# PE held to program order in the first pair of feature tiles of each SwiGLU, and the first half's norm sums issued behind the third product

## The chip, the cores and the metric

The kernel runs on one core of one Trainium2 chip. The metric is the device time of one execution in microseconds, lower being better. The engines are called PE (matrix multiply, with PEld for its weight loads), DVE (vector), ACT (scalar activation), POOL (GpSimd) and SP, which issues the large DMAs.

## What is computed

Two encoder layers run on 560 columns of activations (512 frames, 32 running frames, 16 meta tokens) with a width of 1024. A mixer (gated linear attention in layer 0, latent attention in layer 1) stands between two half-step SwiGLUs in each layer, so there are four SwiGLUs:

```
def rmsnorm(x, w):
    y = x32 * lax.rsqrt(jnp.mean(x32 * x32, axis=-1, keepdims=True) + RMS_EPS)
    return (y * w.astype(jnp.float32)).astype(x.dtype)

def swiglu_half(h, norm_w, w_gate, w_up, w_down):
    hn = rmsnorm(h, norm_w)
    return h + 0.5 * ((jax.nn.silu(hn @ w_gate) * (hn @ w_up)) @ w_down)
```

There are 2816 features, 22 tiles of 128. All matrices are float32.

## The kernel before, in words

Activations lie transposed in `h` (128 partitions, 8 blocks of the width, 560 columns, in two halves of 280). Every weight comes from HBM as float32, and `split` makes two fp32r tiles of it: ACT casts it to `whi` (L331), DVE subtracts to get `wlo` (L332). `mm` then issues high by high (L378) and low by high (L379) in turn, and high by low (L381) behind them.

`gate_up` makes the gate and up projections of a pair of feature tiles by a Strassen-like scheme with seven products instead of eight. A product is two accumulations of twelve matmuls, 24 in all. In the order of the code the products use the operands b11, b21, t6, t5, t7, t4, b22; the text counts them from first (b11) to seventh (b22). Their weights come from the generator `quads`: four quadrants r11, r12, r21, r22, each loaded by two DMAs of 256 KB into a tile `fr` of six buffers, and sums of them made on DVE (L451). The first and second product use r11 and r12 as they are. The third uses r11 + r21 + r22, for which three additions are issued ahead of its cast; the fourth, fifth and sixth use s1, r21 and r22, and the seventh r12 plus the sum. `whi` and `wlo` have four buffers each. In the second to fourth SwiGLU the split weights of the first two products were made in the stage before (`first_weights`); the two quadrants are loaded a second time for the sums.

The products go to the two-bank PSUM tiles A, B and C. `copy` takes a first result to SBUF on ACT (L490). `finish` combines it with a second one on DVE (L497, L499), multiplies by the norm's factor (L501), takes SiLU on ACT (L503), multiplies gate by up (L504) and splits the result into `ah` and `al`.

The norm's factor is applied late, at `finish`. `roots(hf)` sums the squares of a half over the partitions by six matmuls (L410, three column blocks, each of two passes) and makes the reciprocal root by a chain of eleven small DVE instructions of 128x3, each on the result of the one before (L424, L425, then L430, L431, L432 three times). `scale(hf)`, called by the first `finish` of a half, turns the result into a row by three transposes on PE (L417) and copies it to SBUF on ACT (L272).

`first` is true in the first pair of each SwiGLU. There, in the code before, `roots(0)` is issued ahead of the third product, but behind it where `xs.lazy` is set, which is so in the first SwiGLU alone. `finish(0, 0, ...)`, with `scale(0)`, and `roots(1)` are issued behind the fourth product; `scale(1)` comes with the `finish` behind the fifth.

`ffn` goes over five groups of feature tiles. The first group is one pair; from the second on, the down projection of the group before is woven between the products (`between`, `fill`). In the first pair there is nothing to weave in.

The order that each engine runs is made when the program is built. A planner simulates the engines and puts each instruction that is ready on its engine, in the order in which the code emitted them where several are ready. An engine then runs its list strictly in order. The list on PE can so differ from the code's order, as can the lists on DVE and ACT.

Of the kernel before, what the change touches and what calls it, by code (L numbers as in the profile page):

```python
# [2 lines left out]

# [49 lines left out]
def weight_plan():  # L53
# [3 lines left out]
    def ffn(i, l):  # L57
        for gi, (f0, f1) in enumerate(GROUPS):
# [3 lines left out]
            for m in range(ND):  # L62
                plan.append((("d", i, l, gi, m), f1 - f0))

    ffn(1, 0)
    for h in range(GH):
        plan.extend((("v", h, j), nk * V_COLS[h] / P) for j, nk in enumerate(V_PARTS[h]))
# [4 lines left out]
        if h >= 2:  # L72
            plan.extend((("go", h - 2, c), 8) for c in range(4))
    ffn(2, 0)
    ffn(1, 1)
    for m in range(6):
        plan.append((("wd", m), 8))
# [212 lines left out]
class Net:  # L290
# [176 lines left out]
    def gate_up(self, i, l, f, xs, act, raws, tp, between):  # L467


        nc = self.nc  # L470
        v = nc.vector
        n = xs.n
        left = self.quads(i, l, f, raws, xs.early, xs.left)
        done = []

        def product(to, op, more=False):
            if xs.lazy and op in ("b11", "b21"):
                w, x = next(left), xs.operand(op)
            else:
                x, w = xs.operand(op), next(left)  # L480
            for j in range(2):
                self.mm(to[:, j, :n], w, 4 * j, x, (0, n), more)

        def gap():
            done.append(0)
            between(len(done))

        def copy(of, tag):
            r = tp.tile([P, 2, 280], F32, name="r", tag=tag, bufs=1)
            nc.scalar.copy(r[:, :, :n], of[:, :, :n])  # L490
            return r

        def finish(j, hf, bank, r, how):
            gu = tp.tile([P, 2, 280], F32, name="gu", tag="gu", bufs=2)
            b, r, t = bank[:, :, :n], r[:, :, :n], gu[:, :, :n]
            if how == "neg":
                v.scalar_tensor_tensor(t, b, -1.0, r, op0=ALU.mult, op1=ALU.subtract)  # L497
            else:
                v.tensor_tensor(t, b, r, op=how)  # L499
            y = xs.scale(hf).unsqueeze(1).to_broadcast([P, 2, n])  # L500
            v.tensor_tensor(t, t, y, op=ALU.mult)  # L501
            g, u = gu[:, 0, :n], gu[:, 1, :n]
            nc.scalar.activation(g, g, AF.Silu)  # L503
            v.tensor_tensor(g, g, u, op=ALU.mult)  # L504
            c = slice(*xs.halves[hf])
            self.split(act[j][0][:, c], act[j][1][:, c], g)

        first = not xs.finish
        A = self.bank2("A")
        product(A, "b11")  # L510
        r1 = copy(A, "ra")
        gap()
        C = self.bank2("C")
        product(C, "b21")
        if not first:
            finish(0, 0, C, r1, ALU.add)
        gap()
        if first and not xs.lazy:
            xs.roots(0)
        product(A, "t6", True)  # L520
        r2 = copy(A, "rb")
        gap()
        if first and xs.lazy:
            xs.roots(0)
        B = self.bank2("B")
        product(B, "t5")
        p5 = copy(B, "rc")
        if first:
            finish(0, 0, C, r1, ALU.add)
            xs.roots(1)  # L530
        gap()
        product(A, "t7", True)
        r3 = copy(A, "ra")
        finish(1, 1, A, p5, "neg")
        gap()
        D = self.bank2("C")
        product(D, "t4")
        finish(1, 0, D, r3, ALU.subtract)
        gap()
        product(B, "b22", True)  # L540
        finish(0, 1, B, r2, ALU.add)
        gap()
# [19 lines left out]
    def ffn(self, i, l, xs, halves, side, turn):  # L562


        ap, fw = Pools(self.tc, side), Pools(self.tc, side)
        acp = ap(f"act{i}{l}")
        if xs.lazy:
            free = [acp.tile([P, 2, T // 2], F32, name="xt", tag=f"a{x}{j}") for j in range(4, 8) for x in "hl"]
            xs.tmp = [t[:, k, :] for t in free for k in range(2)]
        raws, tp = fw(f"raw{i}{l}", 6), fw(f"tmp{i}{l}", 1)  # L570
        fill = []
        last = len(GROUPS) - 1
        for gi, (f0, f1) in enumerate(GROUPS):
            j0 = 4 * (gi % 2) if gi < last else 0
            acts = [(acp.tile([P, T], F32R, name=f"ah{j}", tag=f"ah{j}"),
                     acp.tile([P, T], F32R, name=f"al{j}", tag=f"al{j}")) for j in range(j0, j0 + 4 if gi == last else j0 + f1 - f0)]
            slots = [7 * min((f1 - f0) // 2, 2) - 1]

            def between(k):
                if slots[0] <= 0 or (slots[0] == 7 * min((f1 - f0) // 2, 2) - 1 and k < 2):  # L580
                    return
                for _ in range(-(-len(fill) // slots[0])):
                    fill.pop(0)()
                slots[0] -= 1

            for f in range(f0, f1, 2):
                if gi == last and f == f0 + 4:
                    assert not fill
                    acts += [(acp.tile([P, T], F32R, name=f"ah{j}", tag=f"ah{j}"),
                              acp.tile([P, T], F32R, name=f"al{j}", tag=f"al{j}")) for j in range(4, 8)]  # L590
                self.gate_up(i, l, f, xs, acts[f - f0:f - f0 + 2], raws, tp, between)
            assert not fill
            order = [(m, hf) for m in range(ND) for hf in (0, 1)]
            if gi < last:
                fill = self.down(i, l, gi, acts, halves, order)
        fw.close()
        after = turn()
        order = Quads.ORDER if isinstance(after, Quads) else (
            [(0, 0), (1, 0), (0, 1), (1, 1), (2, 0), (3, 0), (2, 1), (3, 1)] + [(m, hf) for hf in (0, 1) for m in range(4, 8)])
        for f in self.down(i, l, last, acts, halves, order, after):  # L600
            f()
        ap.close()
# [967 lines left out]
```

## Time and profile before

| | us |
|---|---|
| median of 3 runs | 2114.17 (2113.75 to 2114.99) |
| profiled execution | 2109.41 |
| its span, first to last instruction | 2107.5 |
| PE busy | 2026.0 (96%) |
| DVE busy | 1643.2 (78%) |
| ACT busy | 1018.4 (48%) |

In a timeline row stand the start, the duration, engine, line, operation, tiles and count; a bracket tells the idle time of the engine before it and what ended it. Matmuls overlap, so the step from start to start is what PE spends on one, not the duration.

### The profile page before, as it was taken

To read this page: it belongs to the slowest core of one execution; us is meant where nothing else is said; L and a number is where in the kernel's file an instruction comes from. 1 tells how busy PE (TensorE), PEld (TensorE's weight loads), DVE (VectorE), ACT (ScalarE), POOL (GpSimd) and SP (SyncE) were. 2 spreads that over 40 slices of the span, in tenths; PEclk is the share of its full clock that TensorE was granted. 3 is DMA by queue.
4 is the path that set the end of the run, shared out by engine and by line. 5 is a ranking of instruction groups with operands and counts; after the bars stand their busy time and mean duration, and the time that the engine had idled before them with its cause. 6 is when DMAs were issued, how large, how long until landed. Compare 5 with 4: busy or idle time off the path is not lost.

```text
span 2107.5 us, 38039 instructions
## 1 busy us (share of the span) xinstructions
PE 2026.0 (96%) x15290; PEld 1980.2 (94%) x15290; DVE 1643.2 (78%) x3097; ACT 1018.4 (48%) x1822; POOL 51.4 (2%) x117
## 2 busy tenths in 40 slices
PE   5999999999999899999989999999999979999997
PEld 5999999989999799999979999999988969999997
DVE  8887878556658888788778877886788788878884
ACT  6444445455445444445545444454575454444451
POOL 0000000101110000000000000000210000000000
PEclk8999999999999899999989999999999989999998
DMA  3323222222221332322222322222211223232221
GB/s 131 106 87 107 93 96 78 77 68 71 73 80 55 108 103 82 106 86 91 81 95 96 105 92 91 95 83 92 61 51 59 71 86 100 90 111 91 96 72 62
DMA packets 93633, 183.29 MB, mean 87 GB/s; under 512 B 10433, under 2 KB 22081, under 8 KB 93457
## 3 DMA queue, kind: packets, MB, share of 16 engines
q1 hardware_dynamic: 89632, 176.24, 26.1%
q10 hardware_dynamic: 3824, 4.63, 0.7%
q8 instruction: 120, 1.97, 0.4%
q14 instruction: 57, 0.46, 0.1%
HBM read 176.84 MB, written 3.99 MB: 86 GB/s over the span
## 4 chain that ended last, share of the span: by engine, by line
PE 82%; DVE 10%; ACT 3%; DMA 2%; issue 2%; SPq 0%; POOL 0%; DVEq 0%; ACTq 0%; POOLq 0%
PE Y L381 8%; PE Y L378 8%; PE Y L379 8%; PE A L379 5%; PE A L381 5%; PE A L378 5%; PE ps L378 4%; PE ps L381 4%; PE ps L379 4%; PE B L378 3%; PE B L379 3%; PE B L381 3%; PE C L379 3%; PE C L381 3%; PE C L378 3%; DVE wlo L332 3%
## 5 line engine op out<-in xcount | busy, mean ns | idle before, releaser
L332 DVE TENSOR_TENSOR wlo<-fr,whi 128x1024 fp32r<-128x1024 f32 x302 | 363.9, 1216 | 17.2 <-ACT whi L331 17.0
L378 PE MATMUL Y<-ah,whi 128*128 128x280 f32 (+1 forms) x1408 | 373.8, 291 | 1.9 <-ACT ah L331 1.0
L379 PE MATMUL Y<-ah,wlo 128*128 128x280 f32 (+1 forms) x1408 | 373.4, 292 | 0.0
L331 ACT CAST whi<-fr 128x1024 fp32r<-128x1024 f32 x302 | 313.3, 1049 | 92.9 <-PE C L381 34.6
L378 PE MATMUL A<-x,whi 128*128 128x280 f32 (+1 forms) x1056 | 286.3, 296 | 29.5 <-ACT whi L331 29.5
L379 PE MATMUL A<-x,wlo 128*128 128x280 f32 (+1 forms) x1056 | 285.7, 296 | 1.0 <-DVE wlo L332 1.0
L378 PEld LDWEIGHTS Y<-ah,whi 128*128 128x128 f32 x1408 | 265.2, 188 | 3.4 <-ACT ah L331 1.7
L556 DVE SCALAR_TENSOR_TENSOR h<-Y,h 128x280 f32<-128x280 f32 (+1 forms) x320 | 140.9, 443 | 161.9 <-PE Y L381 161.2
L379 PEld LDWEIGHTS Y<-ah,wlo 128*128 128x128 f32 x1408 | 265.4, 188 | 0.0
L332 DVE TENSOR_TENSOR wlo<-raw,whi 128x512 fp32r<-128x512 f32 (+5 forms) x237 | 203.6, 861 | 76.7 <-ACT whi L331 71.9
L331 ACT CAST whi<-raw 128x512 fp32r<-128x512 f32 (+5 forms) x237 | 176.0, 744 | 173.4 <-PE ps L381 55.2
L381 PE MATMUL Y<-al,whi 128*128 128x280 f32 (+1 forms) x1408 | 233.9, 292 | 0.0
L378 PEld LDWEIGHTS A<-x,whi 128*128 128x128 f32 x1056 | 203.9, 193 | 31.1 <-ACT whi L331 31.1
L451 DVE TENSOR_TENSOR fr<-fr 128x1024 f32<-128x1024 f32 x176 | 214.5, 1219 | 20.4 <-DMA fr<-W 18.1
L379 PEld LDWEIGHTS A<-x,wlo 128*128 128x128 f32 x1056 | 203.7, 193 | 1.7 <-DVE wlo L332 1.4
L381 PEld LDWEIGHTS Y<-al,whi 128*128 128x128 f32 x1408 | 201.2, 189 | 0.0
L378 PE MATMUL B<-x,whi 128*128 128x280 f32 (+1 forms) x704 | 188.6, 293 | 3.4 <-ACT whi L331 3.4
L379 PE MATMUL C<-x,wlo 128*128 128x280 f32 (+1 forms) x704 | 187.1, 292 | 3.5 <-DVE wlo L332 3.5
L379 PE MATMUL B<-x,wlo 128*128 128x280 f32 (+1 forms) x704 | 187.4, 292 | 0.8 <-DVE wlo L332 0.8
L378 PE MATMUL C<-x,whi 128*128 128x280 f32 (+1 forms) x704 | 187.4, 291 | 0.6 <-ACT whi L331 0.6
L381 PE MATMUL A<-x,whi 128*128 128x280 f32 (+1 forms) x1056 | 181.2, 294 | 0.0
L490 ACT COPY r<-A 128x560 f32<-128x560 f32 (+1 forms) x132 | 82.2, 623 | 174.1 <-PE A L381 173.8
(368 smaller groups left out, 4059.2 us busy)
## 6 DMA issues: line engine op xcount, KB each, us to landing
fr<-W SPq DMA_DIRECT2D x352, 256.0 KB, 3.4
raw<-W SPq DMA_DIRECT2D x80, 512.0 KB, 3.5
raw<-W SPq DMA_DIRECT2D x112, 256.0 KB, 2.9
raw<-W SPq DMA_DIRECT2D x40, 128.0 KB, 2.1
h<-xT SPq DMA_DIRECT2D x3, 560.0 KB, 7.6
raw<-W SPq DMA_DIRECT2D x4, 384.0 KB, 3.1
o_y<-h SPq DMA_DIRECT2D x8, 136.0 KB, 2.2
o_y<-h ACTq DMA_DIRECT2D x8, 136.0 KB, 1.9
```

The costliest lines, as they stand in the source:

```text
L331: self.nc.scalar.copy(hi, src)
L332: self.nc.vector.tensor_tensor(lo, src, hi.bitcast(F32), op=ALU.subtract)
L378: f(hi[:, b0 + k, :], xh[:, c], start=not more and k == 0, stop=False)
L379: f(lo[:, b0 + k, :], xh[:, c], start=False, stop=False)
L381: f(hi[:, b0 + k, :], xl[:, c], start=False, stop=k == n - 1)
L451: add = lambda out, x, y: nc.vector.tensor_tensor(out, x, y, op=ALU.add)
L490: nc.scalar.copy(r[:, :, :n], of[:, :, :n])
L556: nc.vector.scalar_tensor_tensor(self.h[:, m, c], Y[:, :n], 0.5, self.h[:, m, c], op0=ALU.mult, op1=ALU.add)
```

## The change

```
         if not first:
             finish(0, 0, C, r1, ALU.add)
         gap()
-        if first and not xs.lazy:
-            xs.roots(0)
         product(A, "t6", True)
         r2 = copy(A, "rb")
         gap()
-        if first and xs.lazy:
+        if first:
             xs.roots(0)
         B = self.bank2("B")
         product(B, "t5")
...
-                self.gate_up(i, l, f, xs, acts[f - f0:f - f0 + 2], raws, tp, between)
+                with self.tc.manual_schedule(engines={mybir.EngineType.PE}) if f == 0 else nullcontext():
+                    self.gate_up(i, l, f, xs, acts[f - f0:f - f0 + 2], raws, tp, between)
```

`manual_schedule` makes PE run what is emitted inside the block in the order of the code. The other engines' order, and where PE instructions from outside the block fall among those inside, stay with the planner. `f == 0` holds once in each SwiGLU. The second part moves `roots(0)` behind the third product in the second to fourth SwiGLU; in the first it already stood there.

## Rows read from the trace of the kernel before

**Rows 1.** The page: busy time by engine.

```profile
PE 2026.0 (96%) x15290; PEld 1980.2 (94%) x15290; DVE 1643.2 (78%) x3097; ACT 1018.4 (48%) x1822; POOL 51.4 (2%) x117
```

**Rows 2.** The waits of PE over the whole span: what waited for what, us in total, times, longest.

```profile
PE A L378 <- ACT whi L331: 29.5, 6, 8.8
PE Y L417 <- DVE ry L432: 21.4, 8, 3.3
```

**Rows 3.** The timeline of PE, second SwiGLU: the first and second product, the norm's sums, the third and fourth product, and the first product of the second pair.

```profile
678.90 0.29 PE L378 MATMUL A<-x,whi 128*128 128x280 f32 x1
...
682.00 0.29 PE L378 MATMUL C<-x,whi 128*128 128x280 f32 x1
...
685.12 0.72 PE L410 MATMUL Y<-ones,acc 128*128 128x1 f32 x6
...
698.23 0.60 PE L378 MATMUL A<-x,whi 128*128 128x280 f32 x1 [3.76 <-ACT whi L331]
...
704.09 0.29 PE L379 MATMUL B<-x,wlo 128*128 128x280 f32 x1
...
716.31 0.29 PE L378 MATMUL A<-x,whi 128*128 128x280 f32 x1
```

**Rows 4.** The timeline of DVE, second SwiGLU: the three additions for the third product with one for the seventh, the split of the seventh, two additions for the second pair, and the split of its first weights.

```profile
693.37 4.99 DVE L451 TENSOR_TENSOR fr<-fr 128x1024 f32<-128x1024 f32 x4
...
705.89 1.23 DVE L332 TENSOR_TENSOR wlo<-fr,whi 128x1024 fp32r<-128x1024 f32 x1 [3.00 <-ACT whi L331]
708.00 2.48 DVE L451 TENSOR_TENSOR fr<-fr 128x1024 f32<-128x1024 f32 x2 [0.88 <-DMA fr<-W]
710.40 1.22 DVE L332 TENSOR_TENSOR wlo<-fr,whi 128x1024 fp32r<-128x1024 f32 x1
```

**Rows 5.** The window view, second SwiGLU, from just ahead of the issue of the quadrants' DMAs (679.10): stretch, its length, busy us of PE, PEld, DVE, ACT, POOL with counts, mean granted PE clock (1.00 is 2.4 GHz, 0.50 is 1.2 GHz), busy share of the DMA engines, GB/s.

```profile
679.00:687.50 8.50, 6.85 (x55) 6.76 (x53) 7.54 (x20) 4.06 (x7) 0.00 (x0) 1.00 0.81 254
...
679.00:689.00 10.00, 7.12 (x58) 7.04 (x57) 8.50 (x26) 4.06 (x7) 0.00 (x0) 1.00 0.81 261
```

**Rows 6.** The timeline of DVE, third SwiGLU: the first half's combination, then the first and last instruction of each of the two chains of the norm.

```profile
1077.25 0.74 DVE L499 TENSOR_TENSOR gu<-C,r 128x560 f32<-128x560 f32 x1 [1.43 <-PE C L381]
1077.91 0.15 DVE L424 TENSOR_SCALAR rv<-Y 128x3 f32<-128x3 f32 x1
...
1079.86 0.16 DVE L432 SCALAR_TENSOR_TENSOR ry<-rt,ry 128x3 f32<-128x3 f32 x1
1081.22 0.16 DVE L424 TENSOR_SCALAR rv<-Y 128x3 f32<-128x3 f32 x1 [1.20 <-PE Y L410]
...
1084.18 0.15 DVE L432 SCALAR_TENSOR_TENSOR ry<-rt,ry 128x3 f32<-128x3 f32 x1
```

**Rows 7.** The window view, third SwiGLU, columns as in rows 5.

```profile
1076.00:1077.00 1.00, 1.00 (x10) 1.00 (x10) 0.00 (x0) 0.00 (x0) 0.00 (x0) 1.00 0.00 0
...
1089.00:1090.00 1.00, 0.60 (x1) 0.29 (x1) 1.00 (x2) 1.00 (x3) 0.00 (x0) 0.50 0.00 0
```

**Rows 8.** The timeline of PE, third SwiGLU: the first instructions of the third product.

```profile
1089.12 0.60 PE L378 MATMUL A<-x,whi 128*128 128x280 f32 x1 [3.76 <-ACT whi L331]
...
1090.46 0.57 PE L379 MATMUL A<-x,wlo 128*128 128x280 f32 x1
```

**Rows 9.** The timelines of DVE and PE, fourth SwiGLU: the additions and the first matmul of the third product.

```profile
1723.48 5.00 DVE L451 TENSOR_TENSOR fr<-fr 128x1024 f32<-128x1024 f32 x4
...
1728.36 0.59 PE L378 MATMUL A<-x,whi 128*128 128x272 f32 x1 [6.17 <-ACT whi L331]
```

**Rows 10.** The window view, fourth SwiGLU, from just ahead of the issue of the quadrants' DMAs (1713.68), columns as in rows 5.

```profile
1713.00:1722.00 9.00, 3.02 (x16) 2.67 (x15) 5.68 (x26) 2.10 (x3) 0.00 (x0) 0.70 0.78 246
```

**Rows 11.** The timeline of PE, first SwiGLU: the third product, the sums of the first half, the sixth product, and the transposes of the second half.

```profile
24.32 0.60 PE L378 MATMUL A<-x,whi 128*128 128x280 f32 x1 [6.43 <-ACT whi L331]
...
30.96 0.72 PE L410 MATMUL Y<-ones,acc 128*128 128x1 f32 x6
31.54 0.38 PE L379 MATMUL B<-x,wlo 128*128 128x280 f32 x1
...
45.90 0.39 PE L379 MATMUL C<-x,wlo 128*128 128x280 f32 x1 [3.49 <-DVE wlo L332]
46.13 0.49 PE L417 MATMUL Y<-ident,ry 128*128 128x128 f32 x3
46.38 0.38 PE L378 MATMUL C<-x,whi 128*128 128x280 f32 x1
```

**Rows 12.** The window view, first SwiGLU, columns as in rows 5.

```profile
24.00:25.00 1.00, 0.60 (x1) 0.29 (x1) 1.00 (x3) 1.00 (x3) 0.00 (x0) 0.50 0.00 0
...
46.00:47.00 1.00, 1.00 (x9) 1.00 (x10) 1.00 (x3) 0.34 (x1) 0.00 (x0) 1.00 0.12 16
```

**Rows 13.** The timeline of DVE, first SwiGLU: the first and last instruction of the two chains of the norm, and the instruction put behind the first one.

```profile
31.72 0.16 DVE L424 TENSOR_SCALAR rv<-Y 128x3 f32<-128x3 f32 x1 [1.64 <-PE Y L410]
31.80 0.45 DVE L400 TENSOR_TENSOR acc<-acc,sq 128x280 f32<-128x280 f32 x1
...
36.05 0.15 DVE L432 SCALAR_TENSOR_TENSOR ry<-rt,ry 128x3 f32<-128x3 f32 x1
...
38.27 0.15 DVE L424 TENSOR_SCALAR rv<-Y 128x3 f32<-128x3 f32 x1
...
45.76 0.15 DVE L432 SCALAR_TENSOR_TENSOR ry<-rt,ry 128x3 f32<-128x3 f32 x1
```

More of the change, by code (lines that the diff above doesn't have):

```diff
@@ L1 @@
-from contextlib import ExitStack
+from contextlib import ExitStack, nullcontext
 from functools import partial
@@ L517, in gate_up @@
         gap()
-        if first and not xs.lazy:
-            xs.roots(0)
         product(A, "t6", True)
@@ L522, in gate_up @@
         gap()
-        if first and xs.lazy:
+        if first:
             xs.roots(0)
@@ L590, in ffn @@
                               acp.tile([P, T], F32R, name=f"al{j}", tag=f"al{j}")) for j in range(4, 8)]
-                self.gate_up(i, l, f, xs, acts[f - f0:f - f0 + 2], raws, tp, between)
+                with self.tc.manual_schedule(engines={mybir.EngineType.PE}) if f == 0 else nullcontext():
+                    self.gate_up(i, l, f, xs, acts[f - f0:f - f0 + 2], raws, tp, between)
             assert not fill
```

## The prediction

> **What bounds the kernel now.** I read the page first: PE is busy for 96% of the span, DVE for 78% [rows 1]. So the kernel is bound by PE, and a change of order can only win back idle PE time or lose more of it. Next come PE's waits [rows 2]. The largest is for the cast of a third product's weights (29.5 us in six cases, the kernel's start among them), and behind it the transposes of the norm's factor, which wait for DVE's chain (21.4 us in eight cases). Both stand in the first pair of a SwiGLU, where no down projection fills in. The timelines of these stretches then show the order. In the second SwiGLU the second product is issued by 685.12, PE makes the sums of *both* halves, and the third product begins at 698.23 [rows 3]. DVE begins the additions for the third product's weights only at 693.37, when the second chain is over [rows 4]. The planner hoisted the second half's sums, which the code emits behind the fourth product, into the idle PE, and the additions came out behind them in DVE's fixed order. The reader is to see that 13.1 us pass there in which PE does nothing but those sums.
>
> **Part one: the additions come earlier.** With PE in program order and `roots(0)` behind the third product, DVE has no chain to run ahead of the additions. What comes last is then the transfer of the quadrants, or DVE's last work before.
>
> *Second SwiGLU.* Eight transfers of 262 KB, 2.10 MB, are needed. By 687.5 the DMAs moved 8.5 us x 254 GB/s = 2.16 MB, by 689.0 2.61 MB, which is all ten that were issued, the next pair's included [rows 5]. So the data are there between 687.3 and 689.0; with some time for the landing I take 688.6. From the start of the additions to the first matmul the trace has 693.37 to 698.23, 4.86 us (three additions, the cast, two handovers). The third product then begins at 693.5 instead of 698.23: 4.8 us won.
>
> *Third SwiGLU.* The DMAs had long been silent at 1076 [rows 7]. DVE is free when L499 ends, 1077.25 + 0.74 = 1078.0, or 0.1 earlier, since the next instruction overlaps it [rows 6]. 1077.9 + 4.9 = 1082.8 against 1089.12 [rows 8]: 6.3 us won. Were the additions put ahead of L499, which waits 1.43 us for PE, it would be 2 us more.
>
> *Fourth SwiGLU.* The additions start at 1723.48 and the product at 1728.36 [rows 9]. Here the DMAs were issued late: by 1722.0 they moved 9 x 246 = 2.21 MB [rows 10]. The data thus landed hardly before the additions began. I take 0.2 us won, with bounds of 0 and 1.7.
>
> *First SwiGLU.* The sums already stood behind the third product, and PE ran them in nearly that order [rows 11]; the first matmuls hoisted there sat in waits. I take 0, bounds of 1 us either way, since a new plan may move things.
>
> Sum: 11.3 us won.
>
> **Part two: the sums no longer hide in the gap.** They now stand between products, on PE's path. Six L410 cost 31.54 - 30.96 = 0.58 us, three L417 46.38 - 46.13 = 0.25 us [rows 11]. That is 0.83 a half, 1.66 a SwiGLU, and 5.0 us in the second to fourth. The 18 + 9 instructions and their operations are the same as before; only their cover goes.
>
> **Part three: the new wait.** In program order `scale(0)`'s transposes stand behind the fourth product, and everything later on PE is queued behind them: the sums of the second half, then the fifth product, then `scale(1)`'s transposes, then the sixth. Each chain must so be done within one product. A product takes 682.00 - 678.90 = 3.1 us [rows 3]. A chain alone takes 1077.91 to 1080.02, 2.1 us, and one that shares DVE with the first half's `finish` 1081.22 to 1084.33, 3.1 us [rows 6]. Either is just hidden. In the first SwiGLU, where DVE always has other work ready, one larger instruction stands between any two of the chain: 31.72 to 36.20, 4.5 us, and 38.27 to 45.91, 7.6 us [rows 13]. By these rows the stall lies between 0 and 1.4 + 4.5 = 5.9 us a SwiGLU.
>
> What would be ready in the second to fourth? A large instruction put into the chain adds its step of 1.14 us less the 0.12 us that the chain leaves free anyway, so 1.0. While the first chain runs, the split of the seventh product's weights comes up, about 1.8 us behind the third product (704.09 to 705.89) [rows 3, 4]: 2.1 + 1.0 = 3.1, a stall of 0.2 with the handover. While the second runs, the first half's `finish` is due, and the split of the second pair's first weights, which followed the fourth product [rows 4], and perhaps one addition for that pair. 3.1 + 1.0, and half of another 1.0, plus 0.1 for the handover, less 3.1: 1.6. I take 1.8 us a SwiGLU, 5.4 in three. It is nearer to the chain with `finish` than to the first SwiGLU, for the operands of the norm are all made by then.
>
> Here a rule of the Trainium skill is weighed. The row shows that the small instruction at 31.72 lasts 0.16 us, but that the next one starts 0.08 us after it [rows 13]; so interleaving costs DVE only half of it. The Trainium skill (VectorE: DVE Perf Modes, "The DRAIN you can't avoid") says that the next operation does not start until the pipeline is empty, though it leaves room for some that start earlier. By the row, the sum stays. By the rule, read strictly, each of eleven would cost 0.08 us more, 0.9 a chain, 5.3 us in six, and the time would be about 2118.5. The trace contradicts it, so that it gets no chance of its own.
>
> **Clock.** The gap before the third product stays long in the second SwiGLU (685.1 to 693.5) and the fourth, so the restart is at 1.2 GHz as before. In the third it shrinks to about 5.6 us (L499's wait for PE ended at 1077.25 [rows 6]). After a wait of 6.43 us the granted clock was 0.50, after one of 3.49 us still 1.00 [rows 11, 12]; 5.6 lies between. The third product there began at 0.50 [rows 7]. A product behind such a gap took 5.9 us from its start instead of 3.1 [rows 3]; of the 2.8, some are a wait for `wlo`. If the clock held, some 2 us would be won. I take 0.
>
> **Sum.** -11.3 + 5.0 + 5.4 = -0.9 us. The profiled execution took 2109.41 (span 2107.5 and 1.9 around it) and would take 2108.5; it lies 4.8 below the median of the timed runs, and I carry the difference over: 2114.2 - 0.9 = 2113.3. The work behind does not take up the stalls: when the first pair ends, the second pair's first weights were split at 711.6, 4.7 us ahead of their product at 716.31 [rows 3, 4], so neither a later PE nor 2 us more of DVE work makes DVE late.
>
> **The rivals.** 0.2% (4.2 us) is what a measurement of this kernel can tell from no change.
>
> 1. *The chains hide.* If the planner runs both chains with little between them, the stalls vanish: -11.3 + 5.0 = -6.3, 2107.9; with the clock held in the third SwiGLU 2105.8. It decides where the stalls stay under 0.7 us a SwiGLU. For it: outside the first SwiGLU the first chain had nothing put between its instructions. Against it: everything ready is put there in the first.
>
> 2. *The chains are held up, slower.* DVE runs its list in order. If the planner, which reckons with its own landing times, puts the second pair's additions into the first chain, the chain waits for their transfers. In the second SwiGLU these additions waited for DMA until 708.00, 9.8 us behind the third product's start, and took 2.4 [rows 4]. The transposes would then be due at about 12.8, while the fourth product ends at 5.9 + 0.6 + 3.1 = 9.6 [rows 3]: a stall of 3.2, and 1.1 for the second chain. 4.3 in each of three is 12.9: -6.3 + 12.9 = +6.6, 2120.8. It decides where the stalls exceed 3.5 us a SwiGLU. Against it: in the order of the code these additions come last, so they go in only where nothing older is ready.
>
> 3. *The change doesn't do what it says*: the additions stay late, for another reason than the chains. Then only PE's cost remains and the same wait is longer: the sums leave a gap that stays, +5.0 or 2119.2. Against it: nothing else stands on DVE between L499 and the additions but the chains and what hangs on them [rows 6].
>
> **How the numbers follow.** Forecast, little change: 0.57. Rival 1: 0.27. Rival 2: 0.12. Rival 3: 0.04. So faster by over 0.2% 0.27, within 0.2% 0.57, slower 0.16. The predicted time is 2113.3. Its own range goes from 2110 to 2118 (stalls of 0.7 to 3.5 us). To leave out no more than two in ten, the range reaches into both rivals: from 2107, with the stalls hidden and about half the chance of the clock, to 2119.
>
> **What will show it.** Right: the L410 rows of the second to fourth SwiGLU behind the third product's 24 matmuls; the additions directly behind L499 and the landing; the third product some 4.8, 6.3 and 0.2 us earlier against the second one than before; PE's wait for L417 down from 21.4 us to some 7. The step most in doubt is the stall at the second half's transposes. Wrong: a wait of over 3 us at L417 in these three, or none at all; additions that still start as late as before; a gain of 2 us or more in the first SwiGLU, for which I have no reason.

## The result, and the profile after

The changed kernel takes 2122.58 us (median of 17 runs, one of which, at 3066.81 us and a granted clock of 0.60, is left out of the ratio) against 2114.50 for the kernel before (17 runs beside them): a ratio of 1.0036, 95% interval 1.0025 to 1.0046. It is slower by some 8 us. The forecast was 2113.3, between 2107 and 2119; it was wrong, on the side to which 0.16 had been given.

The page of the changed kernel hardly differs from [rows 1]; PE is busy 8.5 us more in a span of 2123.6 us, which is 16.1 us longer than that of the profiled execution before.

```profile
PE 2034.5 (96%) x15290; PEld 1986.9 (94%) x15290; DVE 1643.5 (77%) x3097; ACT 1019.0 (48%) x1822; POOL 51.4 (2%) x117
```

PE's waits, to be held against [rows 2] (what waited for what, us in total, times, longest):

```profile
PE A L378 <- ACT whi L331: 44.0, 5, 14.5
PE Y L417 <- DVE ry L432: 12.4, 9, 3.8
...
PE A L378 <- DVE gu L497: 4.4, 3, 1.5
```

The first row is PE's wait for the third product's cast. It has grown from 29.5 to 44.0 us, although the third product comes earlier: before, the sums and transposes lay inside the gap and cut it into pieces. L417's wait went down from 21.4 to 12.4 us, where the prediction looked for 7. In the second to fourth SwiGLU it is 5.0 us in sum, close to the 5.4 forecast there; 3.8 us stand at the second half's transposes of the first SwiGLU, where PE before waited 3.49 us for a `wlo` instead [rows 11]. The third row is new, and the prediction had nothing for it.

The timeline of PE in the second SwiGLU, the rows that answer to [rows 3] (only rows with a wait, the sums and transposes, and the two matmuls behind the first sums):

```profile
698.72 0.60 PE L378 MATMUL A<-x,whi 128*128 128x280 f32 x1 [8.95 <-ACT whi L331]
700.03 0.60 PE L379 MATMUL A<-x,wlo 128*128 128x280 f32 x1 [0.72 <-DVE wlo L332]
...
704.89 0.72 PE L410 MATMUL Y<-ones,acc 128*128 128x1 f32 x6
705.48 0.38 PE L378 MATMUL B<-x,whi 128*128 128x280 f32 x1
705.69 0.29 PE L379 MATMUL B<-x,wlo 128*128 128x280 f32 x1
...
709.86 0.54 PE L417 MATMUL Y<-ident,ry 128*128 128x128 f32 x3 [1.04 <-DVE ry L432]
710.24 0.73 PE L410 MATMUL Y<-ones,acc 128*128 128x1 f32 x6
...
715.64 0.40 PE L378 MATMUL A<-x,whi 128*128 128x280 f32 x1 [1.49 <-DVE gu L497]
...
719.47 0.51 PE L417 MATMUL Y<-ident,ry 128*128 128x128 f32 x3 [0.46 <-DVE ry L432]
```

The order is the one that was forecast as far as 710.24: third product, sums, fourth product, transposes, sums, fifth product. But PE stops three times behind the third product: at the first transposes, at 715.64, and at the second transposes. The matmul of 715.64 is the first product of the *second pair*. It comes from outside the block that is held to program order, and the planner put it ahead of the second half's transposes. Its bank A has to be read by DVE (L497) first.

The timeline of DVE there answers to [rows 4]:

```profile
690.31 0.73 DVE L499 TENSOR_TENSOR gu<-C,r 128x560 f32<-128x560 f32 x1
693.84 5.00 DVE L451 TENSOR_TENSOR fr<-fr 128x1024 f32<-128x1024 f32 x4 [2.79 <-DMA fr<-W]
...
705.65 0.16 DVE L424 TENSOR_SCALAR rv<-Y 128x3 f32<-128x3 f32 x1 [2.27 <-PE Y L410]
...
707.31 1.22 DVE L332 TENSOR_TENSOR wlo<-fr,whi 128x1024 fp32r<-128x1024 f32 x1
...
708.52 1.22 DVE L451 TENSOR_TENSOR fr<-fr 128x1024 f32<-128x1024 f32 x1
709.65 0.15 DVE L432 SCALAR_TENSOR_TENSOR ry<-rt,ry 128x3 f32<-128x3 f32 x1
709.77 1.23 DVE L451 TENSOR_TENSOR fr<-fr 128x1024 f32<-128x1024 f32 x1
...
711.56 0.15 DVE L424 TENSOR_SCALAR rv<-Y 128x3 f32<-128x3 f32 x1
711.63 1.21 DVE L332 TENSOR_TENSOR wlo<-fr,whi 128x1024 fp32r<-128x1024 f32 x1
...
713.20 1.21 DVE L451 TENSOR_TENSOR fr<-fr 128x1024 f32<-128x1024 f32 x1
...
714.85 0.74 DVE L497 SCALAR_TENSOR_TENSOR gu<-A,r 128x560 f32<-128x560 f32 x1
...
715.79 1.22 DVE L332 TENSOR_TENSOR wlo<-fr,whi 128x1024 fp32r<-128x1024 f32 x1
...
717.05 1.22 DVE L451 TENSOR_TENSOR fr<-fr 128x1024 f32<-128x1024 f32 x1
...
719.16 0.16 DVE L432 SCALAR_TENSOR_TENSOR ry<-rt,ry 128x3 f32<-128x3 f32 x1
```

The additions (693.84) now stand right behind the combination of the first half (690.31) and wait for nothing but their data, as forecast. Then the reader is to see what lies inside the chains. The first (L424 at 705.65 to the end of L432 at 709.80, 4.1 us) holds a split of 1.22 us and an addition for the second pair, and the next addition (709.77) stands ahead of L501. The second runs from 711.56 to 719.32, 7.8 us for eleven instructions that take 2.1 alone: between them lie two splits and two additions of 1.2 us, L497 and more. No row inside the chains has a wait for DMA.

Two marks in each SwiGLU give the account. "End" is the first matmul of the sixth product of the second pair, where the changed order has passed. The times are us from the first matmul of the SwiGLU's first product, read from PE's timeline.

| | third product, before → after | end, before → after | end, difference |
|---|---|---|---|
| second SwiGLU | 19.32 → 15.34 | 58.28 → 60.55 | +2.3 |
| third | 18.35 → 12.00 | 58.05 → 58.18 | +0.1 |
| fourth | 21.71 → 20.63 | 59.97 → 66.17 | +6.2 |

The sum, 8.6 us, agrees with the loss between the medians, 8.1. The two profiled executions differ by 16.1 us; the other 7.5 lie outside these stretches, 1.3 of them in the first SwiGLU. Differences of that size come without a change of order: a2 below, which runs the same instructions in the same order as the kernel before, took 6.6 us more than it in its profiled execution, and no more in these three stretches. The third product did come earlier, by 4.0, 6.4 and 1.1 us, 11.4 in sum; behind it 20.0 us were lost. The next table takes the steps from start to start on PE behind the third product's first matmul apart. A step beyond the full-clock one (0.126 us with 280 columns, 0.1245 with 272) is put down to the instruction that came late; the figures are after less before.

| us, behind the third product's start | second | third | fourth | sum | predicted |
|---|---|---|---|---|---|
| sums and transposes on PE's path | 1.8 | 2.1 | 2.1 | 6.0 | 5.0 |
| stalls: transposes, and the second pair's first product | 3.5 | 3.5 | 3.9 | 10.9 | 5.4 |
| the third product's wait for its `wlo` | 0.4 | 0.4 | 0.4 | 1.1 | 0 |
| all other matmul steps | 0.6 | 0.5 | 0.9 | 2.0 | 0 |

Of the last row 1.1 us are the first matmuls behind sums, transposes and stalls, four in a SwiGLU: their step is 0.21 us or a little more instead of 0.126, at a granted clock of 1.00 (705.48 to 705.69 above). 0.5 us are matmuls at a granted clock of 0.50, and the rest is spread over many steps.

### The profile page after: what moved, and what is told of

It is laid out like the page before. It is cut to its first block, busy times and chain, and to the rows that moved or that the text cites. A ratio compares the mean times of both kernels' runs of the same rounds, so it can differ in the third digit from the quotient of the medians.

```text
span 2123.6 us, 38032 instructions
## 1 busy us (share of the span) xinstructions
PE 2034.5 (96%) x15290; PEld 1986.9 (94%) x15290; DVE 1643.5 (77%) x3097; ACT 1019.0 (48%) x1822; POOL 51.4 (2%) x117
## 4 chain that ended last, share of the span: by engine, by line
PE 84%; DVE 9%; DMA 2%; ACT 2%; issue 2%; SPq 0%; POOL 0%; DVEq 0%; ACTq 0%; POOLq 0%
PE Y L381 8%; PE Y L378 8%; PE Y L379 8%; PE A L379 6%; PE A L381 6%; PE A L378 5%; PE ps L378 4%; PE ps L381 4%; PE ps L379 4%; PE C L379 4%; PE C L378 4%; PE C L381 3%; PE B L379 3%; PE B L381 3%; PE B L378 3%; DVE wlo L332 3%
## 5 line engine op out<-in xcount | busy, mean ns | idle before, releaser
L451 DVE TENSOR_TENSOR fr<-fr 128x1024 f32<-128x1024 f32 x176 | 214.5, 1219 | 28.6 <-DMA fr<-W 25.9
```

Of the source, the lines that this page charges most:

```text
L451: add = lambda out, x, y: nc.vector.tensor_tensor(out, x, y, op=ALU.add)
```

## The experiments

Each ran beside the kernel before on its chip. The sum of the differences at the "end" in the second to fourth SwiGLU, against the profile of before, is given for each as "stretches"; 4.2 us are 0.2%.

| run | stretches, us | ratio to before, 95% interval |
|---|---|---|
| the change | +2.3 +0.1 +6.2 | 1.0036 (1.0025 to 1.0046) |
| a1_order_alone | +1.6 +0.8 +4.9 | 1.0037 (1.0024 to 1.0051) |
| a2_sums_alone | 0.0 -0.3 +0.2 | 1.0005 (0.9994 to 1.0017) |
| a3_not_in_first | | 1.0048 (1.0031 to 1.0065) |
| a4_short_chain | -2.3 -4.9 +2.3 | 0.9990 (0.9979 to 1.0001) |
| d1_paired_chains_behind | 0.0 -3.4 +3.8 | 0.9999 (0.9987 to 1.0011) |
| b1_both_sums_ahead | -2.9 -2.8 +0.5 | 0.9983 (0.9970 to 0.9995) |
| e1_sums_ahead_planned | -0.4 0.0 +0.2 | 1.0000 (0.9987 to 1.0012) |
| c4_short_chain_on_before | -1.2 -1.6 +0.5 | 0.9986 (0.9974 to 0.9998) |
| g1_one_chain_behind_additions | -3.0 -5.2 +1.0 | 0.9958 (0.9944 to 0.9971) |
| g2_one_chain_planned | -3.5 -5.5 +0.9 | 0.9960 (0.9945 to 0.9974) |

**Each part alone.** a1 keeps `roots(0)` where it was and only puts PE in program order; a2 moves `roots(0)` and leaves PE to the planner.

```
 a2:
-        if first and not xs.lazy:
-            xs.roots(0)
         product(A, "t6", True)
...
-        if first and xs.lazy:
+        if first:
             xs.roots(0)
```

> Part one of the change alone: PE in program order in the first pair, the first half's sums ahead of the third product again (behind it in the first SwiGLU, as ever). Measure: from the first matmul of a SwiGLU's first product to the first one of the second pair's sixth product; before 70.3, 58.3, 58.1, 60.0 us, with the whole change 71.6, 60.6, 58.2, 66.2. Theory S (the sums on PE's path, some 1.8 us a SwiGLU, and DVE chains stretched by large instructions, some 3.7 us, eat what the earlier third product wins): the first chain hides in the gap, so 0.6 + 1.3 us less than the whole change in the second and fourth SwiGLU; in the third the additions come 2 us later, so no gain there; the second chain is stretched as before. Time 2118.5, ratio to before about 1.0018. Rival O (program order on PE costs, wherever the sums stand): as the whole change, 1.0036.

> Part two alone: the first half's sums are emitted behind the third product in all stages, PE left to the planner. Theory S: nothing holds the sums back, the planner hoists them into the idle PE as it does with the second half's; all four stretches as before (70.3, 58.3, 58.1, 60.0), ratio 1.0000 within 0.0010. Rival M (moving the sums is what costs): the stretches of the second and fourth SwiGLU at least 1.5 us longer, ratio 1.0015 or more.

a2 does nothing: the planner moves the sums back into the gap, and its order on PE, DVE and ACT is that of before, instruction for instruction. What the change does, it so does by the program order. a1 is as slow as the change; there theory S missed, and the time is the one that rival O had named (b1 below, in program order and faster than the kernel before, speaks against its reason). The fourth product hides the first chain there (no wait at the first transposes), but the second half's grew:

```profile
709.05 0.40 PE L378 MATMUL A<-x,whi 128*128 128x280 f32 x1 [1.49 <-DVE gu L497]
...
714.14 0.54 PE L417 MATMUL Y<-ident,ry 128*128 128x128 f32 x3 [1.73 <-DVE ry L432]
```

1.49 us for L497 and 1.73 at the second transposes: what the first chain no longer costs, the second one does. Large work that is ready on DVE goes into whichever chain is open.

**Program order outside the first SwiGLU alone.**

```
-                with self.tc.manual_schedule(...) if f == 0 else nullcontext():
+                with self.tc.manual_schedule(...) if f == 0 and not xs.lazy else nullcontext():
```

> The whole change, but in the first SwiGLU PE is left to the planner. Theory S: the first stretch goes back from 71.6 to 70.3 us, the other three stay at 60.6, 58.2, 66.2; ratio about 1.0030. Rival N (the 1.3 us there are noise of one execution): the first stretch stays near 71.6, ratio 1.0036.

1.0048, with an interval that overlaps that of the change: with the first SwiGLU left to the planner the loss stays, so it does not arise there. (Of this run only the times are used.)

**A shorter chain, on the change and on the kernel before.** The three Newton steps are left out in the SwiGLUs, which leaves two of eleven instructions; that part of the norm's computation is missing in both runs.

```
-        self.finish[hf] = self.net.roots(hf, c1 - c0, D)
+        self.finish[hf] = self.net.roots(hf, c1 - c0, D, 0)
```

> The whole change with the three refinement steps of the reciprocal root left out in the SwiGLUs: the chain has 2 instructions instead of 11, and part of the norm's computation is missing. Theory S: the sums stay on PE's path, but PE no longer waits at the transposes, and the second pair's first product no longer goes ahead of them; 3.7 us less in each of the second to fourth stretch (about 56.9, 54.5, 62.5), time about 2111.5, ratio 0.9985. Rival P (the PE time of the sums and a colder clock are the loss, the waits only cover what would be waited for anyway): under 1 us less a stretch, ratio 1.0025 or more.

> The kernel before with the chains of the SwiGLUs cut from eleven instructions to two (the Newton steps are left out, so part of the norm's computation is missing): the control for the short chain on the change, which was 0.9990. Theory K: the chains alone hold the additions back in the code before; with short ones the third product comes about 3.5 us earlier in the second and third SwiGLU and the same in the fourth; ratio to before 0.997, so the change still costs some 4 us against it, the sums on PE's path. Rival: the chains' length does not decide before, since the additions wait for something else; ratio 1.000.

On the change, the waits at the transposes are gone in the second to fourth SwiGLU, the second pair's first product is no longer put ahead, and the ratio falls from 1.0036 to 0.9990, by 9.7 us. That the chains make the stalls is so shown. The same cut wins 3.0 us on the kernel before (0.9986), so that with short chains the two orders can't be told apart. On the kernel before, theory K missed by half: the third product came 1.9 and 1.3 us earlier in the second and third SwiGLU, not 3.5, and the 4 us by which the change with short chains was to be slower than this run did not show. Chains of before were 2.1 and 3.1 us long; shortening them doesn't bring the additions to L499. What still stands ahead of them is told by the next runs.

**The chains moved, at the same cost on PE.** d1 is the change with the second half's sums directly behind the first half's, both behind the third product.

```
         if first:
             xs.roots(0)
+            if not xs.lazy:
+                xs.roots(1)
```

> The whole change, but the second half's sums stand directly behind the first half's, both behind the third product: PE pays the same 1.8 us of sums and transposes a SwiGLU, only the second chain is begun one product earlier. Theory K: the first transposes wait about 1 us, the second ones not at all; the second to fourth SwiGLU get 2 to 3 us shorter each against the change, ratio to before 0.9995 to 1.001. Rival P (what costs is the sums' own time on PE and the restart of PE at a lower clock): the same as the change, ratio 1.0036.

The timeline of PE in d1, second SwiGLU (waits, sums and transposes):

```profile
693.90 0.60 PE L378 MATMUL A<-x,whi 128*128 128x280 f32 x1 [8.99 <-ACT whi L331]
695.22 0.60 PE L379 MATMUL A<-x,wlo 128*128 128x280 f32 x1 [0.72 <-DVE wlo L332]
...
700.17 1.40 PE L410 MATMUL Y<-ones,acc 128*128 128x1 f32 x12
...
705.98 0.51 PE L417 MATMUL Y<-ident,ry 128*128 128x128 f32 x3 [1.21 <-DVE ry L432]
...
709.39 0.49 PE L417 MATMUL Y<-ident,ry 128*128 128x128 f32 x3
```

0.9999: the two chains, begun together, cost 1.2 us at the first transposes and nothing at the second, and no product of the second pair is put ahead. With as many instructions on PE as the change has, 3.7 in a thousand are won back, and the stretches are 2.3, 3.5 and 2.4 us shorter than the change's. Theory K was right, rival P is out. It is the place of the second chain that made the change slower than the kernel before. The sums and transposes still take 1.8 us of PE a SwiGLU in d1, and with the first transposes' wait they eat what the earlier third product wins: d1 is no faster than before either.

**Both sums ahead, with and without program order.** b1 puts both halves' sums in front of the third product and holds PE to program order in the second to fourth SwiGLU; e1 is the same with PE left to the planner.

```
         if first and not xs.lazy:
             xs.roots(0)
+            xs.roots(1)
         product(A, "t6", True)
...
-            xs.roots(1)
+            if xs.lazy:
+                xs.roots(1)
```

> Program order on PE in the first pair of the second to fourth SwiGLU, with both halves' sums ahead of the third product, so that the two chains alternate on DVE right behind the first half's combination and ahead of the additions. Theory K (what costs is that large DVE instructions get between the instructions of a chain on which PE waits): the chains end in DVE's idle time, the transposes never wait, and the additions start as soon as data and DVE allow. Against before the stretch up to the second pair's sixth product gets shorter by about 4 us in the second SwiGLU, 3.5 in the third (the additions there start some 2.2 us behind the first half's combination) and 0 in the fourth; ratio to before 0.9965, about 2107. Rival O (program order on PE costs by itself, because PE may no longer fill its waits with other products): the loss of 2 to 3 us a SwiGLU behind the third product stays; ratio 0.9995 to 1.002.

> Both sums ahead of the third product as in the run with both sums ahead, but PE's order left to the planner. Theory K: the chain pair is about 2 us shorter than the two chains of before, and the additions start about 2 us earlier in the second and third SwiGLU, 0 in the fourth; ratio to before 0.998, so that about half of the gain needs no program order. Rival O: without program order all of the gain comes, ratio 0.9965, as the first half's combination work that stays ahead of the additions runs while their data are under way.

The timelines of DVE in b1 and then in e1, second SwiGLU (e1's first two rows are the same as b1's):

```profile
691.81 0.73 DVE L499 TENSOR_TENSOR gu<-C,r 128x560 f32<-128x560 f32 x1
692.46 0.22 DVE L424 TENSOR_SCALAR rv<-Y 128x3 f32<-128x3 f32 x2
...
694.41 0.23 DVE L432 SCALAR_TENSOR_TENSOR ry<-rt,ry 128x3 f32<-128x3 f32 x2
695.02 5.01 DVE L451 TENSOR_TENSOR fr<-fr 128x1024 f32<-128x1024 f32 x4 [0.37 <-DMA fr<-W]
```

```profile
694.42 0.24 DVE L432 SCALAR_TENSOR_TENSOR ry<-rt,ry 128x3 f32<-128x3 f32 x2
695.70 0.74 DVE L501 TENSOR_TENSOR gu<-gu,yn 128x560 f32<-128x560 f32 x1 [1.05 <-ACT yn L272]
696.95 0.45 DVE L504 TENSOR_TENSOR gu<-gu 128x280 f32<-128x280 f32 x1 [0.50 <-ACT gu L503]
697.89 0.45 DVE L332 TENSOR_TENSOR al<-gu,ah 128x280 fp32r<-128x280 f32 x1 [0.49 <-ACT ah L331]
698.25 5.00 DVE L451 TENSOR_TENSOR fr<-fr 128x1024 f32<-128x1024 f32 x4
```

In both, the chains of the two halves alternate (x2) and are over at 694.65. In b1 the additions follow at 695.02, when their data are there; the transposes never wait again in these three, and 0.9983 comes out. That is half of the gain that theory K had named (0.9965): the third product came 4.2, 3.7 and 0.2 us earlier, and some 1 us a SwiGLU was lost again behind it. In e1 the planner ran the transposes at once, and with them the rest of the first half's `finish` became ready: L501, L504 and the split of `al`, each waiting about 0.5 to 1 us for ACT. The additions stand behind that, at 698.25; the third product comes 0.1 to 1.0 us earlier, and no time is won (1.0000 where theory K said 0.998). So the additions of the kernel before are held back by chains *and* the `finish` that hangs on them; b1 gains because program order keeps the transposes, and so the `finish`, behind the fourth product.

**The order on DVE set instead.** g1 and g2 make one chain of 128x6 for both halves. Its sums stand ahead of the third product, and DVE is held to program order over that product, so that the additions come ahead of the chain. (The chain made for both halves and the order on DVE were changed together; no run has the one without the other.) g1 holds PE as well, g2 leaves PE to the planner.

```
+        early = first and not xs.lazy
+        if early:
+            xs.sums()
+        with self.tc.manual_schedule(engines={mybir.EngineType.DVE}) if early else nullcontext():
             product(A, "t6", True)
+            if early:
+                xs.chain()
```

> PE in program order in the first pair of the second to fourth SwiGLU; both halves' sums ahead of the third product, one chain of eleven 128x6 instructions for both halves, and DVE held to program order over the third product, so that its additions come ahead of that chain. Theory K2 (two places cost: large DVE instructions ahead of the additions, and a chain that PE waits for): the third product comes as early as in the change or earlier, 14.9 us, 12.0 and 21.4 us behind the first one, and the chain is over before the fourth product is. Against before about -3.5, -5.5 and +0.4 us in the second to fourth SwiGLU; ratio 0.996. Rival (the third SwiGLU's gain is given back to something else, the restart of PE or the second pair's transfers): as with both sums ahead, 0.998.

> The same sums, the same chain and the same order on DVE, but PE's order left to the planner, which begins the fourth product while the third one waits for its second weight tile. Theory K2: the order on DVE is what the gain needs, not that on PE: about 0.4 to 0.8 us a SwiGLU less than with PE in program order, -4, -6 and 0 us in the second to fourth; ratio 0.9955. Rival O (program order on PE is what brings the gain): the transposes or later products get ahead as in the code before and the third product comes late again; ratio 1.000.

DVE and then PE of g2 in the third SwiGLU (the lines have moved: L499 is L522, L451 is L474, the sums are L434 and the transposes L439):

```profile
1073.25 0.74 DVE L522 TENSOR_TENSOR gu<-C,r 128x560 f32<-128x560 f32 x1 [1.42 <-PE C L385]
1073.91 4.99 DVE L474 TENSOR_TENSOR fr<-fr 128x1024 f32<-128x1024 f32 x4
...
1079.95 0.16 DVE L447 TENSOR_SCALAR rv<-Y 128x6 f32<-128x6 f32 x1
...
1084.97 0.17 DVE L455 SCALAR_TENSOR_TENSOR ry<-rt,ry 128x6 f32<-128x6 f32 x1
```

```profile
1072.99 1.39 PE L434 MATMUL Y<-ones,acc 128*128 128x1 f32 x12
1078.77 0.60 PE L382 MATMUL A<-x,whi 128*128 128x280 f32 x1 [4.38 <-ACT whi L335]
1079.72 0.60 PE L382 MATMUL B<-x,whi 128*128 128x280 f32 x1 [0.35 <-ACT whi L335]
...
1088.55 0.49 PE L439 MATMUL Y<-ident,ry 128*128 128x128 f32 x3
...
1091.95 0.49 PE L439 MATMUL Y<-ident,ry 128*128 128x128 f32 x3
```

The sums lie in the gap, the additions stand right behind the combination, the chain has three splits between its instructions and is yet over at 1085.1, 3.4 us ahead of its transposes, which don't wait. Both versions beat the kernel before, 2105.83 and 2106.51 us against 2116.19 beside them, and so the changed one. g1 and g2 can't be told apart by time, so the expected advantage of the planned order on PE is not shown there (in the profiles g2 is 0.1 to 0.5 us a SwiGLU ahead). But rival O is out: program order on PE is not needed for the gain.

## Why the prediction was wrong

*The additions.* Right: 4.0, 6.4 and 1.1 us won against 4.8, 6.3 and 0.2, and 11.4 against 11.3 in sum. The data of the second SwiGLU were estimated right as the last to come: its additions wait for DMA. The reading of [rows 4] was too short, though. The text made the chain the last thing ahead of the additions; e1 and c4 show that the first half's `finish` is, once its transposes have run.

*The sums on PE.* 6.0 us against 5.0. The first half's sums stand behind a product that runs at a granted clock of 0.50 in the third and fourth SwiGLU, and took 0.87 and 0.81 us there (steps to the next matmul) instead of 0.59. The first half's transposes took 0.38 us (709.86 to 710.24) where the prediction had read 0.25 off [rows 11].

*The stalls.* This is the step that failed: 10.9 us against 5.4, 3.6 a SwiGLU against 1.8. The prediction's chains were 3.1 and 4.6 us long; they took 4.1 and 7.8. The chains of [rows 13] had shown what happens where DVE has other work ready, 4.5 and 7.6 us, and the prediction set them aside because the operands are all made by then. Of the second to fourth SwiGLU it counted one large instruction for the first chain and one and a half for the second. The second SwiGLU had two and four of 1.2 us, with L497, L504 and a split of `al` besides: the splits and additions of the second pair are as good a filler as operands. The length that follows, 7.8 us, is near that of the first SwiGLU's second chain, 7.6, though there the instructions between were mostly of 0.45 us [rows 13] and here of 1.2. The upper bound, 5.9 us, held; the value was taken too near to the low end.

*A step left out.* The second pair's first product lies outside the block, and the prediction did not ask where the planner would put it. It went ahead of the second half's transposes and waited for bank A, 1.6 us of the 3.6. No run shows the same chain without it; by the rows the transposes, free to start at some 714.0, would then have waited for the chain's end at 719.3. So the long chain, and not this product, is taken to be what cost the time.

*Program order and the wait for the third product's `wlo`.* The third product's second matmul waits for `wlo` (it stands at 1090.46 in [rows 8]; 700.03 in the timeline above). In the kernel before, the fourth product's first matmul was put into that wait, 0.95 us behind the third's first (698.23 in [rows 3]); in program order nothing may, and the step is 1.32 us. Some 0.4 us a SwiGLU were not in the sum.

```profile
699.18 0.60 PE L378 MATMUL B<-x,whi 128*128 128x280 f32 x1 [0.35 <-ACT whi L331]
```

*The clock.* The third product of the third SwiGLU was thought possibly to keep the full clock behind a gap of 5.6 us. It did not: the gap was 5.61 us and the clock 0.50. The forecast had taken 0 for it. The matmuls at the lower clock cost 0.5 us more than before, and the first matmuls behind sums, transposes and stalls 1.1 at the full clock; the sum had neither.

```profile
1089.16 0.60 PE L378 MATMUL A<-x,whi 128*128 128x280 f32 x1 [5.61 <-ACT whi L331]
```

*The rivals.* The time came out near where rival 2 had put it (2120.8), and the stalls at its point (3.5 us), but not by its mechanism. Additions of the second pair did get into the first chain (708.52), but neither they nor any instruction of the chains waited for a transfer. It is the number of large instructions put between, not their waiting. Rival 3 is out, since the additions came early. Rival 1, hidden chains, did not come in the change; b1, g1 and g2 make it true by another order. Its -6.3 us can't be held against b1's -5.2: in b1 the sums lie in the gap as well, and the third SwiGLU's third product comes 2.7 us later than in the change.

*The rule weighed.* By the Trainium skill (VectorE: DVE Perf Modes, "The DRAIN you can't avoid"), read strictly, more small instructions cost their full length. b1 shows 22 of them, two chains in turn, in 694.65 - 692.46 = 2.2 us, where eleven alone take 2.1 [rows 6]. The row was the right thing to go by.

## What to carry to other kernels

A chain of short dependent instructions costs what the other work on its engine puts between them, not its own length; so count everything that is ready there, of the next stage too, before a second engine is made to wait for it in a fixed order. Where one engine's order is the fault, set it on that engine: here DVE's additions were late. Program order on PE brought the third products forward by 11.4 us in sum, but lost 6.7 us a SwiGLU behind them; in g2 the order on DVE, with one chain for both halves, brought them forward by 10.9 and lost 0.9. Sums that feed a chain belong into an idle stretch well ahead of its use.

## What the runs showed of the hardware

A second chain costs almost nothing if it alternates with the first: 2.2 us for both against 2.1 for one, in b1 and in e1. The window view shows PE's clock (the number after POOL's columns) behind a gap of 4.38 us in g2's third SwiGLU:

```profile
1079.00:1080.00 1.00, 0.65 (x2) 0.34 (x2) 1.00 (x2) 1.00 (x2) 0.00 (x0) 0.50 0.00 0
```

It is 0.50 there, as it is behind 5.61 us. Behind 3.49 us it was still 1.00 in the kernel before [rows 11, 12], but 0.50 in b1 behind a wait of the same length at the same matmul (timeline, then window view), so that the prediction's reading of that row, clock kept, was one of two outcomes:

```profile
48.15 0.60 PE L379 MATMUL C<-x,wlo 128*128 128x280 f32 x1 [3.49 <-DVE wlo L332]
```

```profile
48.00:49.00 1.00, 0.85 (x4) 0.85 (x5) 1.00 (x5) 0.00 (x0) 0.00 (x0) 0.50 0.00 0
```

The first SwiGLU has two outcomes with one and the same order on PE, DVE and ACT. From its first product to the end mark it took 70.2 and 70.3 us in g2 and before, and 74.2 to 75.0 in a2, b1, e1 and g1. The window of 45 to 65 us in before and then in b1:

```profile
45.00:65.00 20.00, 16.07 (x103) 15.08 (x104) 18.38 (x28) 8.20 (x16) 0.00 (x0) 0.91 0.19 60
```

```profile
45.00:65.00 20.00, 14.40 (x64) 13.73 (x65) 15.66 (x28) 6.29 (x12) 0.00 (x0) 0.66 0.17 59
```

The granted clock is 0.91 in the one and 0.66 in the other. They part at the wait of 3.49 us: behind it the clock was 1.00 in g2 as in before, and 0.50 in a2, e1 and g1 as in b1. What decides between them was not tried. It is as large as the effects studied here, and it is one reason to compare stretches as well as totals.
